# High and low rows of w_up in one matmul of 512 columns, in a hybrid decoder layer on one Trainium2 core

## The chip, the cores and the metric

The kernel runs on one core of one Trainium2 chip. A core has TensorE (matmuls; PE in the profile, PEld for its weight loads), VectorE (DVE), ScalarE (ACT), GpSimd (POOL) and SyncE (SP), each with a queue of its own that it works off in order, and 16 DMA engines. The metric is the device time in microseconds, the median of several runs.

## The reference

One decoder layer for 512 tokens behind 16 meta tokens, model width 2048, in float32:

```
u    = rmsnorm(h, norm_mix)
proj = u @ w_in                        # attention and mLSTM inputs
mix  = [sliding-window attention with sinks | chunkwise mLSTM]
h    = h + mix @ w_out
u    = rmsnorm(h, norm_mlp)
h    = h + square(relu(u @ w_up)) @ w_down     # 2048 -> 8192 -> 2048
out  = rmsnorm(h, norm_final)[without meta tokens]
```

The change is in `u @ w_up`, where each product is 512 tokens x 2048 x 8192.

## The kernel before, in words

**Precision.** TensorE takes operands in fp32r. To keep float32 accuracy each operand is split in a high part (the value cast to fp32r, by ACT, line 118) and a low part (the rest, by DVE, line 119), in `split`. A product a x w is then three matmuls: high by high, low by high, high by low.

**Stages, in order of time.** The input projection (lines 165, 178 to 180, 227), attention and mLSTM between its tiles, w_out (lines 709 to 711, `tok_gemm`), w_up (`up_quad`, lines 755 to 757), w_down (`product` and `step`, lines 1056 to 1060), and the final norm. In w_out and w_down the weights' halves stream through TensorE in 512 columns and activations are the loaded operand; in w_up the weights (`whi`, `wlo`, 128x128 at a time) are loaded and the activations stream.

**w_up.** It is done in 32 quads. A quad takes a 2 x 2 arrangement of blocks and works it with seven products instead of eight (the sums and differences of Strassen's scheme in Winograd's form): the weight sums `s1` to `s4` are made by DVE (`w_sum`, line 735), the activation sums were made before, when the rows were transposed. `ORDER = (0, 1, 5, 4, 6, 2, 3)` is the order of the products. Each product runs over KQ = 8 slices q of 128 rows, with three matmuls of HTOK = 256 columns per slice: `wh` by `yh`, `wh` by `yl`, `wl` by `yh`. Results lie in three PSUM tiles, X, W and Q (W and Q are halves of one bank), and X and Q go on accumulating over several products; ACT copies X or Q out in between, DVE adds, and ACT applies Relu and Square to the tile `d` (four quarters of 256 columns). DVE makes four sums `fs` of d (POOL does so in the last quad), and ACT's queue sends d and fs to DRAM (lines 824, 825). Odd quads use the PSUM tiles named a, even ones g. Quad 0 is written by hand and overlaps with the end of w_out.

**Buffers.** `hi_lo` gives a pair of weight halves from three buffers each (`whi`, `wlo`). The activations yh, yl of j = 0, 1 lie in the pool b2, those of j = 2, 3 in slots of the pool xpool, which are reused: x in the input projection, the attention output in w_out, y in w_up, and the first 16 of 24 places for the units of w_down. A slot is TOK = 528 elements wide. The other 8 places are in the pool b3r (tiles named r). Slots of xpool appear in the profile as s; so do the weight sums of w_up and of w_down, which are also named s.

**w_down.** Units (512-column pieces of d and fs, read back from DRAM, tile fu) are split into high and low halves and used as the loaded operand; the weights come in blocks as raw and rh, with DVE's differences t1 to t4 (`weight_sum`, line 1025). Its pools are opened when those of w_up close, one behind the other in the space that the pool b2 (y tiles, then weight sums) and the pool b2b (d, fs, raws, small ones) leave: b3f (fu, rh), b3r, b3 (the quarters c), b3s (weight sums s).

**Order.** Where nothing else is said, a planner decides the order of instructions on each engine's queue from a priority (the program's order) and a timeline of its own. In `manual_schedule` blocks the program's order stands for the engines named: all of w_down's loop on PE, ACT and DVE. The last product (g = LAST + 12), written in two halves t, stood outside of such a block.

Of the kernel before, what the change touches and what calls it, by code (L numbers as in the profile page):

```python
# [10 lines left out]
F32 = mybir.dt.float32  # L11
F32R = mybir.dt.float32r
AF = mybir.ActivationFunctionType
ALU = mybir.AluOpType
# [69 lines left out]
def hybrid_layer(ctx, tc, io, out):  # L84
# [100 lines left out]
    with tc.tile_pool(name="a0", bufs=1) as a0:  # L185
# [15 lines left out]
        for k0, kn in groups:  # L201
            xr = a0.tile([P, kn, TOK], F32, name=f"xr{k0}")
            wr = (mk[:, :, :SEQ], mq, qa[0], qa[1])[k0 // 4][:, k0 % 4 : k0 % 4 + kn]
            sync.dma_start(out=xr[:], in_=io["xt"][:, k0 : k0 + kn])
            sync.dma_start(out=wr, in_=io["wa"][:, k0 : k0 + kn])
            if k0 == 1:
                sync.dma_start(out=cst[:, KT:], in_=io["cst"][:, KT:])
            for j in range(kn):
                kt = k0 + j
                xh[kt], xl[kt] = xslot(2 * kt, (P, TOK)), xslot(2 * kt + 1, (P, TOK))  # L210
# [365 lines left out]
    def mlstm_block(n):  # L576
# [30 lines left out]
        for h in range(MH):  # L607
            o = abank((P, MV + 1))
            pe.matmul(o[:], e[:, h], ml["v"][:, n, h], start=True, stop=False)
            pe.matmul(o[:], qs[:, h], ml["C"][:, h], start=False, stop=True)  # L610
            act.copy(num[:, h], o[:])
            act.activation(junk[:], num[:, h, :MV], AF.Square, accum_out=ss[:, h : h + 1])
# [64 lines left out]

    ah, al = [None] * KT, [None] * KT
    for kt in range(KT):
        ah[kt], al[kt] = xslot(2 * kt, (P, SEQ)), xslot(2 * kt + 1, (P, SEQ))  # L680
# [35 lines left out]

    b2s = ExitStack()
    b2 = b2s.enter_context(tc.tile_pool(name="b2", bufs=1, reuse_waits="tile"))
    yh, yl = {}, {}
    for p in ORDER:  # L720
        for j in range(2):
            yh[p, j] = b2.tile([P, 2, HTOK], F32R, name=f"yh{p}_{j}")
            yl[p, j] = b2.tile([P, 2, HTOK], F32R, name=f"yl{p}_{j}")

    def sum_tile():
        return b2.tile([P, 1024], F32, name="s", tag="s", bufs=NS_)
# [2 lines left out]
    def operand(src):  # L729
        w = hi_lo()  # L730
        split(w[0][:], w[1][:], src)
        return w
# [4 lines left out]
    def up_quad(quad):  # L737
# [10 lines left out]
        s1, s2, s3, s4 = (sum_tile() for _ in range(4))  # L748
        nb = abank if quad % 2 else bank

        def product(p, w, out, q0=0, q1=KQ, start=True):
            for q in range(q0, q1):
                wh, wl = (t[:, q * P : (q + 1) * P] for t in w)
                ah_, al_ = yh[p, q // 2][:, q % 2], yl[p, q // 2][:, q % 2]
                pe.matmul(out, wh, ah_, start=start and q == 0, stop=False, skip_group_check=True)  # L755
                pe.matmul(out, wh, al_, start=False, stop=False, skip_group_check=True)  # L756
                pe.matmul(out, wl, ah_, start=False, stop=q == KQ - 1, skip_group_check=True)  # L757

        if quad == 0:
            pa, pb, pc = (nb((P, 2, HTOK)) for _ in range(3))  # L760
# [29 lines left out]
            act.activation(d[:], d[:], AF.Relu)  # L790
        else:

            X, B = nb((P, HTOK)), nb((P, 2, HTOK))
            W, Q = B[:, 0], B[:, 1]
            d = b2b.tile([P, 4, HTOK], F32, name="d", bufs=2)
# [4 lines left out]
            product(1, operand(x12), W)  # L800
            product(5, operand(s2[:]), X[:], start=False)
            dve.tensor_tensor(out=d[:, 0], in0=d[:, 0], in1=W, op=ALU.add)  # L802
            act.copy(d[:, 2], X[:])
            product(4, operand(s1[:]), Q)
            w_sum(s3, x11, x21, ALU.subtract)
            act.copy(d[:, 1], Q)
            product(6, operand(s3[:]), X[:], start=False)
            w_sum(s4, x12, s2[:], ALU.subtract)
            act.copy(d[:, 3], X[:])
            product(2, operand(s4[:]), Q, start=False)  # L810
            dve.tensor_tensor(out=d[:, 3], in0=d[:, 3], in1=d[:, 1], op=ALU.add)
            act.activation(d[:, 0], d[:, 0], AF.Relu)
            product(3, operand(x22), X[:], start=False)
            dve.tensor_tensor(out=d[:, 2], in0=d[:, 2], in1=Q, op=ALU.add)
            act.activation(d[:, 2:4], d[:, 2:4], AF.Relu)
            act.activation(d[:, 1], X[:], AF.Relu)
        act.activation(d[:], d[:], AF.Square)
        fs = b2b.tile([P, 4, HTOK], F32, name="fs")
        summer = dve if quad < NQ - 1 else pool
# [9 lines left out]
    with tc.tile_pool(name="b2a", bufs=1, reuse_waits="tile") as b2a:  # L829
        for j in range(NJ):  # L830
# [55 lines left out]
                act.activation(y[:, i], src, AF.Copy, scale=gmlp[:, kt : kt + 1])  # L886
            if j >= 2:
                for i, p in enumerate(ORDER):
                    yh[p, j] = xslot(4 * i + 2 * (j - 2), (P, 2, HTOK))
                    yl[p, j] = xslot(4 * i + 2 * (j - 2) + 1, (P, 2, HTOK))  # L890
# [34 lines left out]
    b3r = []  # L925


    def unit_slot(k, n, shape, dt=F32R):
        k %= UNITS
        if k < 16:  # L930
            i = 2 * XU[k] + n
            return xpool.tile(list(shape), dt, tag=f"s{i}", name=f"s{i}")
        return b3r[0].tile(list(shape), dt, tag=f"r{k}_{n}", name=f"r{k}_{n}")

    keys_ = [(c, p, h) for c in range(NC) for p in ORDER for h in range(2)]
    loaded, unit = {}, {}
# [4 lines left out]
        sync.dma_start(out=buf[:].rearrange("p (a b) -> p a b", a=2), in_=fdram[2 * c + h][pos // 4][:, pos % 4])  # L941

    def split_unit(k, buf):
        unit[keys_[k]] = hi, lo = [unit_slot(k, n, (P, 512)) for n in range(2)]
        split(hi[:], lo[:], buf[:])

    def early_unit(buf):
        k = len(loaded)
# [25 lines left out]


    b3f = ctx.enter_context(tc.tile_pool(name="b3f", bufs=1, reuse_waits="tile"))
    b3r.append(ctx.enter_context(tc.tile_pool(name="b3r", bufs=1, reuse_waits="tile")))
    b3 = ctx.enter_context(tc.tile_pool(name="b3", bufs=1, reuse_waits="tile"))
    b3s = ctx.enter_context(tc.tile_pool(name="b3s", bufs=1, reuse_waits="tile"))
    dps = ctx.enter_context(tc.tile_pool(name="dps", bufs=1, space=PSUM, reuse_waits="tile"))  # L980

    def f_buffer():
# [123 lines left out]
            sync.dma_start(out=nfs[j][:], in_=io["nf"][:, j * 512 : (j + 1) * 512])  # L1106

    def load_h1(row, j):
        for b in (2 * row, 2 * row + 1):
            h1[b, j] = unit_slot(len(keys_) + 2 * j + b // 2, b % 2, (P, 512), F32)[:]  # L1110
            sync.dma_start(out=h1[b, j], in_=hd[j][row][:, b % 2])

    def load_quarter(row, col):
# [4 lines left out]

    def squares(row, j):
        for b in (2 * row, 2 * row + 1):  # L1120
            square_sum(junk[:], b, j, h1[b, j])

    def weigh(row, j):
        for b in (2 * row, 2 * row + 1):
# [58 lines left out]

    def last_square(b, j):
        last_sq[b] = b3.tile([P, 1], F32, name=f"sq{b}")
        act.activation(junk[:], h1[b, j], AF.Square, accum_out=last_sq[b][:])

    load_units(FB)
    load_rows0(0, 0)
    load_rows0(0, 1)  # L1190
    load_rows1(0)
    junk = unit_slot(len(keys_) + 2 * NJ, 0, (P, 512), F32)
# [108 lines left out]
```

## Time and profile before

| what | value |
|---|---|
| median of 3 runs | 2002.85 us (2001.46 to 2003.85) |
| the profiled execution | 1999.89 us, its span 1998.1 us |
| granted TensorE clock, mean | 0.996 |
| PE busy | 1971.5 us, 99% of the span, 12240 matmuls |
| DVE busy | 1405.5 us, 70% |
| ACT busy | 1011.1 us, 51% |
| POOL busy | 236.0 us, 12% |
| w_up, quads 1 to 31 | 735 us to 1358 us from the span's start |
| w_down | 1358 us to the end |

Matmuls are pipelined: a row of one lasts longer than the time until the next begins, so the price of a matmul is the time from start to start. A group's row reads: line, engine, operation, written tile <- read tiles, shape, count, then busy us, mean ns of one, idle us ahead of it and who ended that. A row of the timeline reads: start, duration, engine, line, operation, tiles, shape, and in brackets the idle time ahead of it with its releaser. A row of waits reads: who waited, for whom, us in total, times, the longest.

### The profile page before, as it was taken

The numbers are of one execution on the slowest core, as the hardware profiler recorded it, in microseconds if no ns is written. First come the engines' busy times: TensorE is split into PE (matmuls) and PEld (weight loads), VectorE is DVE, ScalarE is ACT, GpSimd is POOL, SyncE is SP. The second block draws the span as 40 slices with busy tenths as digits, with TensorE's granted clock in tenths as the row PEclk, the third lists the DMA queues.
The fourth block names the chain that finished last, engine by engine and source line by source line (L and its number), as shares of the span: only waits on it lengthen the run. The fifth ranks groups of instructions, "written<-read, shape, count | busy, mean of one in ns | idle before, by whom it ended". The sixth has DMA issues, their size and how long they took to land.

```text
span 1998.1 us, 30652 instructions
## 1 busy us (share of the span) xinstructions
PE 1971.5 (99%) x12240; PEld 1754.5 (88%) x12240; DVE 1405.5 (70%) x1844; ACT 1011.1 (51%) x1491; POOL 236.0 (12%) x341
## 2 busy tenths in 40 slices
PE   9999999999999999999999999998999999999997
PEld 7878889988888889999999999997888888888886
DVE  6557673233643478877777777776888888888878
ACT  4433552235533355555555555555566565555655
POOL 0112220012120023122220000000100000010011
PEclk9999999999999999999999999999999999999999
DMA  8412112221343336555554444456887887787766
GB/s 313 132 64 87 64 64 85 85 85 64 106 148 129 108 146 208 192 183 187 183 186 158 161 156 162 156 167 216 206 223 211 227 222 211 218 216 194 219 170 188
DMA packets 113392, 324.61 MB, mean 162 GB/s; under 512 B 14016, under 2 KB 51008, under 8 KB 94288
## 3 DMA queue, kind: packets, MB, share of 16 engines
q1 hardware_dynamic: 66304, 246.60, 36.1%
q0 software_dynamic: 11856, 40.38, 10.6%
q10 hardware_dynamic: 35088, 35.66, 5.5%
q8 instruction: 96, 1.57, 0.3%
q14 instruction: 48, 0.39, 0.1%
HBM read 244.45 MB, written 78.15 MB: 161 GB/s over the span
## 4 chain that ended last, share of the span: by engine, by line
PE 90%; issue 4%; DVE 2%; DMA 1%; ACT 1%; POOL 1%; DVEq 0%; SPq 0%; POOLq 0%; ACTq 0%
PE g L165 10%; PE a L755 5%; PE a L757 5%; PE a L756 5%; PE g L755 5%; PE g L757 5%; PE g L756 5%; PE X L1056 5%; PE X L1060 5%; PE X L1059 5%; PE g L709 3%; PE g L711 3%; PE g L710 3%; PE Q L1060 2%; PE Q L1056 2%
## 5 line engine op out<-in xcount | busy, mean ns | idle before, releaser
L118 ACT CAST whi<-raw 128x1024 fp32r<-128x1024 f32 x224 | 234.9, 1049 | 412.3 <-PE g L711 89.6
L119 DVE TENSOR_TENSOR wlo<-raw,whi 128x1024 fp32r<-128x1024 f32 x224 | 274.2, 1225 | 207.1 <-ACT whi L118 201.8
L119 DVE TENSOR_TENSOR wlo<-s,whi 128x1024 fp32r<-128x1024 f32 x256 | 312.9, 1223 | 121.6 <-ACT whi L118 119.5
L118 ACT CAST whi<-s 128x1024 fp32r<-128x1024 f32 x256 | 268.7, 1050 | 224.8 <-PE g L756 64.1
L165 PE MATMUL g<-s,whi 128*128 128x264 f32 x1216 | 205.1, 287 | 0.2 <-DVE qa L263 0.2
L165 PEld LDWEIGHTS g<-s,whi 128*128 128x128 f32 x1216 | 171.0, 189 | 5.4 <-issue 4.9
L1060 PE MATMUL X<-whi,s 128*128 128x512 f32 x356 | 140.2, 394 | 0.0
L1056 PE MATMUL X<-whi,s 128*128 128x512 f32 x356 | 140.0, 393 | 0.0
L1059 PE MATMUL X<-wlo,s 128*128 128x512 f32 x356 | 139.8, 393 | 0.0
L165 PE MATMUL g<-s,wlo 128*128 128x264 f32 x608 | 128.0, 287 | 0.0
L755 PE MATMUL a<-yh,whi 128*128 128x256 f32 x448 | 126.5, 282 | 1.5 <-DVE d L802 0.8
L755 PE MATMUL g<-yh,whi 128*128 128x256 f32 x448 | 126.7, 283 | 1.2 <-ACT whi L118 1.1
L757 PE MATMUL a<-yh,wlo 128*128 128x256 f32 x448 | 126.4, 282 | 0.6 <-DVE wlo L119 0.6
L757 PE MATMUL g<-yh,wlo 128*128 128x256 f32 x448 | 126.2, 282 | 0.0
L755 PE MATMUL a<-s,whi 128*128 128x256 f32 x448 | 126.1, 282 | 0.0
L756 PE MATMUL g<-yl,whi 128*128 128x256 f32 x448 | 126.1, 281 | 0.0
L756 PE MATMUL a<-yl,whi 128*128 128x256 f32 x448 | 126.1, 281 | 0.0
L755 PE MATMUL g<-s,whi 128*128 128x256 f32 x448 | 125.8, 282 | 0.0
L757 PE MATMUL a<-s,wlo 128*128 128x256 f32 x448 | 125.7, 280 | 0.0
L757 PE MATMUL g<-s,wlo 128*128 128x256 f32 x448 | 125.6, 281 | 0.0
L756 PE MATMUL a<-s,whi 128*128 128x256 f32 x448 | 125.5, 280 | 0.0
L756 PE MATMUL g<-s,whi 128*128 128x256 f32 x448 | 125.4, 280 | 0.0
(367 smaller groups left out, 5114.0 us busy)
## 6 DMA issues: line engine op xcount, KB each, us to landing
raw<-in_w_dram SPq DMA_DIRECT2D x144, 1024.0 KB, 5.1
rh<-in_w_dram SPq DMA_DIRECT2D x64, 512.0 KB, 5.3
hd<-c POOLq DMA_DIRECT2D x61, 512.0 KB, 5.5
fu<-fd SPq DMA_DIRECT2D x110, 256.0 KB, 3.5
fd<-d ACTq DMA_DIRECT2D x32, 512.0 KB, 3.2
fd<-fs ACTq DMA_DIRECT2D x32, 512.0 KB, 3.5
xtok<-in_x_dram SPq DMA_DIRECT2D x4, 1024.0 KB, 11.5
hs<-in_x_dram SPq DMA_DIRECT2D x16, 256.0 KB, 6.0
```

The lines of the kernel that those rows point to most:

```text
L118: act.copy(dst_hi, src)
L119: dve.tensor_tensor(out=dst_lo, in0=src, in1=dst_hi.bitcast(F32), op=ALU.subtract)
L165: pe.matmul(ps[s][:], w, x[:, s * HALF : (s + 1) * HALF], start=first and kt == 0, stop=last and kt == KT - 1,)
L709: pe.matmul(ps[b][:], a, wh, start=kt == first, stop=False)
L710: pe.matmul(ps[b][:], a, wl, start=False, stop=False)
L711: pe.matmul(ps[b][:], c, wh, start=False, stop=kt == last)
L755: pe.matmul(out, wh, ah_, start=start and q == 0, stop=False, skip_group_check=True)
L756: pe.matmul(out, wh, al_, start=False, stop=False, skip_group_check=True)
L757: pe.matmul(out, wl, ah_, start=False, stop=q == KQ - 1, skip_group_check=True)
L1056: pe.matmul(out[:, t], a, wh[:, cols], start=start and h == q == 0, stop=False, skip_group_check=True)
L1059: pe.matmul(out[:, t], a, wl[:, cols], start=False, stop=False, skip_group_check=True)
L1060: pe.matmul(out[:, t], a2, wh[:, cols], start=False, stop=h == q == 1, skip_group_check=True)
```

## The change

Slots for high and low halves become one tile with both (`xpair`, `unit_pair`, `y_pair`): one tile of [128, 2, n] per pair. For y it is `[P, 2, 2, HTOK]` (half, slice, token), so that one access pattern reads a slice's high and low rows as two runs of 256 columns. In quads 1 to 31 `wide` streams both in one matmul of 512 columns for `wh`; `wl` still takes the high rows alone. The result of a product is then two halves of one bank, and X, W and Q are a bank each. `snapshot` copies both halves out (tile e), and DVE adds the halves, partly ahead of and partly behind the other sums. The early Relus of single quarters become one Relu over all of d. The tile d has one buffer instead of two, e has two of half its size. The pool b3s is opened right behind b3f instead of last. The last product's two halves are in a `manual_schedule` block for PE.

```diff
-    def xslot(i, shape):
-        return xpool.tile(list(shape), F32R, tag=f"s{i}", name=f"s{i}")
+    def xpair(i, shape, dt=F32R):
+        t = xpool.tile([P, 2] + list(shape), dt, tag=f"s{i}", name=f"s{i}")
+        return t[:, 0], t[:, 1]
...
+    def y_pair(p, j, pool_, **kw):
+        ys[p, j] = t = pool_.tile([P, 2, 2, HTOK], F32R, **kw)
+        yh[p, j], yl[p, j] = t[:, 0], t[:, 1]
...
-        def product(p, w, out, q0=0, q1=KQ, start=True):
+        def product(p, w, out, q0=0, q1=KQ, start=True, wide=False):
             for q in range(q0, q1):
                 wh, wl = (t[:, q * P : (q + 1) * P] for t in w)
...
+                if wide:
+                    pe.matmul(
+                        out[:], wh, ys[p, q // 2][:, :, q % 2], start=start and q == 0, stop=False,
+                        skip_group_check=True,
+                    )
+                    pe.matmul(out[:, 0], wl, ah_, start=False, stop=q == KQ - 1, skip_group_check=True)
...
-            X, B = nb((P, HTOK)), nb((P, 2, HTOK))
-            W, Q = B[:, 0], B[:, 1]
-            d = b2b.tile([P, 4, HTOK], F32, name="d", bufs=2)
-            product(0, operand(x11), X[:])
-            act.copy(d[:, 0], X[:])
+            X, W, Q = (nb((P, 2, HTOK)) for _ in range(3))
+            d = b2b.tile([P, 4, HTOK], F32, name="d")
+            def snapshot(src):
+                e = b2b.tile([P, 2, HTOK], F32, name="e", bufs=2)
+                act.copy(e[:], src[:])
+                return e
...
+            wide(0, x11, X)
+            e0 = snapshot(X)
             w_sum(s1, x21, x22, ALU.add)
             w_sum(s2, s1[:], x11, ALU.subtract)
...
+            wide(1, x12, W)
+            wide(5, s2[:], X, False)
+            add(e0[:], e0[:], W[:])
+            e2 = snapshot(X)
+            wide(4, s1[:], Q)
             w_sum(s3, x11, x21, ALU.subtract)
...
+            add(d[:, 0], e0[:, 0], e0[:, 1])
+            act.copy(d[:, 1], Q[:, 0])
+            add(d[:, 1], d[:, 1], Q[:, 1])
+            wide(6, s3[:], X, False)
             w_sum(s4, x12, s2[:], ALU.subtract)
...
+            e3 = snapshot(X)
+            wide(2, s4[:], Q, False)
+            add(d[:, 3], e3[:, 0], e3[:, 1])
+            add(d[:, 3], d[:, 3], d[:, 1])
+            wide(3, x22, X, False)
+            add(e2[:], e2[:], Q[:])
+            add(d[:, 2], e2[:, 0], e2[:, 1])
+            act.copy(d[:, 1], X[:, 0])
+            add(d[:, 1], d[:, 1], X[:, 1])
+            act.activation(d[:], d[:], AF.Relu)
         act.activation(d[:], d[:], AF.Square)
...
     b3f = ctx.enter_context(tc.tile_pool(name="b3f", bufs=1, reuse_waits="tile"))
+    b3s = ctx.enter_context(tc.tile_pool(name="b3s", bufs=1, reuse_waits="tile"))
     b3r.append(ctx.enter_context(tc.tile_pool(name="b3r", bufs=1, reuse_waits="tile")))
     b3 = ctx.enter_context(tc.tile_pool(name="b3", bufs=1, reuse_waits="tile"))
-    b3s = ctx.enter_context(tc.tile_pool(name="b3s", bufs=1, reuse_waits="tile"))
...
-        product(LAST + 12, (t,), (0, 1))
+        with tc.manual_schedule(engines=MAN):
+            product(LAST + 12, (t,), (0, 1))
```

More of the change, by code (lines that the diff above doesn't have):

```diff
@@ L718, in hybrid_layer @@
     b2 = b2s.enter_context(tc.tile_pool(name="b2", bufs=1, reuse_waits="tile"))
[L719 removed]
+    ys, yh, yl = {}, {}, {}
+    def y_pair(p, j, pool_, **kw):
+        ys[p, j] = t = pool_.tile([P, 2, 2, HTOK], F32R, **kw)
+        yh[p, j], yl[p, j] = t[:, 0], t[:, 1]
     for p in ORDER:
         for j in range(2):
[L722 to L723 removed]
+            y_pair(p, j, b2, name=f"y{p}_{j}")
     def sum_tile():
@@ L749, in up_quad @@
         nb = abank if quad % 2 else bank
-        def product(p, w, out, q0=0, q1=KQ, start=True):
+        def product(p, w, out, q0=0, q1=KQ, start=True, wide=False):
             for q in range(q0, q1):
                 wh, wl = (t[:, q * P : (q + 1) * P] for t in w)
[L754 to L757, printed above, removed]
+                ah_ = yh[p, q // 2][:, q % 2]
+                if wide:
[4 more added lines that the diff above has]
+                    pe.matmul(out[:, 0], wl, ah_, start=False, stop=q == KQ - 1, skip_group_check=True)
+                else:
+                    pe.matmul(out, wh, ah_, start=start and q == 0, stop=False, skip_group_check=True)
+                    pe.matmul(out, wh, yl[p, q // 2][:, q % 2], start=False, stop=False, skip_group_check=True)
+                    pe.matmul(out, wl, ah_, start=False, stop=q == KQ - 1, skip_group_check=True)
         if quad == 0:
@@ L791, in up_quad, with wide @@
         else:
-            X, B = nb((P, HTOK)), nb((P, 2, HTOK))
-            W, Q = B[:, 0], B[:, 1]
-            d = b2b.tile([P, 4, HTOK], F32, name="d", bufs=2)
-            product(0, operand(x11), X[:])
-            act.copy(d[:, 0], X[:])
+            X, W, Q = (nb((P, 2, HTOK)) for _ in range(3))
+            d = b2b.tile([P, 4, HTOK], F32, name="d")
+            def wide(p, src, out, start=True):
+                product(p, operand(src), out, start=start, wide=True)
+            def snapshot(src):
+                e = b2b.tile([P, 2, HTOK], F32, name="e", bufs=2)
+                act.copy(e[:], src[:])
+                return e
@@ L798, in up_quad, with add @@
+            def add(dst, in0, in1):
+                dve.tensor_tensor(out=dst, in0=in0, in1=in1, op=ALU.add)
+            wide(0, x11, X)
+            e0 = snapshot(X)
             w_sum(s1, x21, x22, ALU.add)
             w_sum(s2, s1[:], x11, ALU.subtract)
[L800 to L804, printed above, removed]
+            wide(1, x12, W)
@@ L810, in up_quad @@
[L810 to L816, printed above, removed]
+            e3 = snapshot(X)
+            wide(2, s4[:], Q, False)
@@ L925, in hybrid_layer, with unit_pair @@
     b3r = []
-    def unit_slot(k, n, shape, dt=F32R):
+    def unit_pair(k, dt=F32R):
         k %= UNITS
         if k < 16:
-            i = 2 * XU[k] + n
-            return xpool.tile(list(shape), dt, tag=f"s{i}", name=f"s{i}")
-        return b3r[0].tile(list(shape), dt, tag=f"r{k}_{n}", name=f"r{k}_{n}")
+            return xpair(XU[k], (512,), dt)
+        t = b3r[0].tile([P, 2, 512], dt, tag=f"r{k}", name=f"r{k}")
+        return t[:, 0], t[:, 1]
     keys_ = [(c, p, h) for c in range(NC) for p in ORDER for h in range(2)]
@@ L943, in split_unit @@
     def split_unit(k, buf):
-        unit[keys_[k]] = hi, lo = [unit_slot(k, n, (P, 512)) for n in range(2)]
-        split(hi[:], lo[:], buf[:])
+        unit[keys_[k]] = hi, lo = unit_pair(k)
+        split(hi, lo, buf[:])
     def early_unit(buf):
```

21 lines of the change are left out of this document (9 added, 12 removed).

## The prediction

> **What bounds the kernel now.** I read the page first, then the table by stretches, then the waits inside the w_up stretch, then single rows.
>
> ```profile
> span 1998.1 us, 30652 instructions
> PE 1971.5 (99%) x12240; PEld 1754.5 (88%) x12240; DVE 1405.5 (70%) x1844; ACT 1011.1 (51%) x1491; POOL 236.0 (12%) x341
> PE 90%; issue 4%; DVE 2%; DMA 1%; ACT 1%; POOL 1%; DVEq 0%; SPq 0%; POOLq 0%; ACTq 0%
> ```
>
> TensorE (PE) carries 90% of the chain that ended last, so what shortens its stream shortens the run, as long as no other engine takes over. The table by stretches says where that could happen (start:end, length, then busy time of PE, weight load, DVE, ACT, POOL, granted clock):
>
> ```profile
> 735.00:764.00 29.00, 26.92 (x220) 26.12 (x219) 26.79 (x35) 16.07 (x22) 16.09 (x8) 1.00 0.45 152
> 764.00:1358.00 594.00, 593.82 (x4995) 593.61 (x4994) 459.45 (x533) 318.80 (x447) 62.27 (x86) 1.00 0.52 176
> 1358.00:1372.00 14.00, 6.50 (x28) 5.04 (x27) 5.88 (x8) 6.94 (x10) 2.87 (x4) 0.87 0.40 113
> ```
>
> The middle row is w_up: 594.00 us over 4995 matmuls is 118.9 ns from one to the next, with no holes. A quad has 7 products x 8 slices x 3 = 168 matmuls, so it lasts 19.98 us; 594.00 holds 29.73 quads. In each, DVE is busy 459.45/29.73 = 15.45 us and idle 4.52. Is that idle time slack or need? The waits of the same stretch answer:
>
> ```profile
> DVE wlo L119 <- ACT whi L118: 116.9, 119, 1.9
> ACT whi L118 <- PE g L756: 107.5, 75, 1.9
> ACT whi L118 <- PE a L756: 107.2, 74, 1.6
> ```
>
> DVE waits for ACT's casts, and ACT for PE to give back a weight buffer: 116.9 of DVE's 134.5 us idle is PE's own pace. It can be filled.
>
> **The change part by part.**
>
> *w_up in 512 columns.* In quads 1 to 31 each slice goes from three matmuls of 256 columns to one of 512 (wh over high and low rows together) and one of 256 (wl over high): 31 x 7 x 8 = 1736 slices. w_down already runs 512 columns, here with weights from the tiles r and from s:
>
> ```profile
> 1411.85 0.40 PE L1056 MATMUL W<-whi,s 128*128 128x512 f32 x1
> ...
> 1417.39 0.40 PE L1056 MATMUL X<-whi,s 128*128 128x512 f32 x1
> 1500.00 0.39 PE L1056 MATMUL Q<-whi,r 128*128 128x512 f32 x1
> ...
> 1510.88 0.39 PE L1056 MATMUL Q<-whi,s 128*128 128x512 f32 x1
> ```
>
> From 1411.85 to 1417.39 is one product of 24 matmuls: 230.8 ns each. From 1500.00 to 1510.88 are 48: 226.7 ns. Twice 118.9 is 237.8, so a 512 in place of two 256 saves 7.0 to 11.1 ns. In w_up the loaded weights are whi and wlo, the same in all slices, and half of the rows lie in plain tiles, half in s; I take 228, nearest to the r rows. A slice then costs 228 + 118.9 = 346.9 instead of 356.7, a quad 19.43, and 1736 x 9.8 ns = **-17.1 us** (-12.2 to -19.3).
>
> The Trainium skill, "TensorE: Matmul & The Clock Gate", section Back-to-back issue gap, gives N/2.4 + 2.5 ns for a warm matmul by itself; that is 109.2 and 215.8 ns, so joining would save 2.5 ns a slice, an estimated 4.3 us in place of 17.1. The trace does not agree with it: a 256 takes 118.9 here, so more than that rule's fixed part goes when one instruction goes.
>
> *Halves added on leaving PSUM.* ACT and DVE pay. Three DVE adds of 256 columns per quad (L802, L811, L814) become two of 512 and six of 256. Rows of quad 0 have both sizes, two of them reading PSUM; the cost in the queue is from start to start:
>
> ```profile
> 741.96 0.41 DVE L788 TENSOR_TENSOR d<-fs,g 128x256 f32<-128x256 f32 x1
> 742.29 0.68 DVE L789 TENSOR_TENSOR d<-fs,g 128x512 f32<-128x512 f32 x1
> 742.89 0.41 DVE L802 TENSOR_TENSOR d<-d,a 128x256 f32<-128x256 f32 x1
> 743.22 1.21 DVE L119 TENSOR_TENSOR wlo<-s,whi 128x1024 fp32r<-128x1024 f32 x1
> L118 ACT CAST whi<-s 128x1024 fp32r<-128x1024 f32 x118 | 124.1, 1051 | 128.8 <-PE g L756 63.1 <-PE a L756 61.8
> L119 DVE TENSOR_TENSOR wlo<-s,whi 128x1024 fp32r<-128x1024 f32 x118 | 144.3, 1223 | 70.1 <-ACT whi L118 68.2
> L815 ACT ACTIVATE d<-d 128x512 f32<-128x512 f32 x30 | 18.8, 626 | 0.0
> L812 ACT ACTIVATE d<-d 128x256 f32<-128x256 f32 x30 | 12.6, 419 | 8.1 <-DVE d L802 8.1
> L816 ACT ACTIVATE d<-g 128x256 f32<-128x256 f32 x15 | 5.7, 377 | 0.0
> L809 ACT COPY d<-a 128x256 f32<-128x256 f32 x15 | 5.5, 364 | 0.0
> L817 ACT ACTIVATE d<-d 128x1024 f32<-128x1024 f32 x29 | 30.8, 1061 | 0.9
> ```
>
> 256 columns cost 0.33, 512 cost 0.60. So 2 x 0.60 + 6 x 0.33 = 3.18 against 0.99: +2.2 us. DVE goes to 17.65 of a quad of 19.43, 91%, with 1.78 us left. ACT: three copies of 512 at about 0.63 (L815's size), two of 256 at 0.36 and a Relu of 1024 at 1.06 in place of four copies of 256 and Relus of 0.42, 0.63 and 0.38: +0.8 on 318.80/29.73 = 10.7 us. Both stay under PE, so in the steady state I cost them at nothing; DVE's cover is the 1.78 us. Three weight buffers help: a buffer is cast when PE leaves it, two products (5.5 us) before its next use, and cast plus subtraction take 1.05 + 1.22 us, so DVE may come 3.2 us late before PE feels it. New waits of PE are those of X and Q: each is copied or added out while another product of 2.8 us runs.
>
> *One d instead of two.* The quad's first write to d must now wait until the last quad's d has gone to DRAM:
>
> ```profile
> 1015.63 0.28 PE L755 MATMUL a<-yh,whi 128*128 128x256 f32 x1
> 1020.22 1.06 ACT L817 ACTIVATE d<-d 128x1024 f32<-128x1024 f32 x1
> 1021.42 0.52 ACTq L824 DMA_DIRECT2D fd<-d  x1
> DMA to landing us min/median/max: 3.2/3.2/5.2
> POOL fs L820 <- ACT d L817: 316.7, 1, 316.7
> ```
>
> The next quad's products began at 1015.63 (the tile names turn from g to a), so the issue of d comes 5.8 us in. The new end of a quad (copy 0.36, add 0.42, whole Relu 1.06 in place of the last Relu of 0.38) makes it 7.3, landing at 10.5. The first sum into d is ready at about 6.5: DVE can block there for up to 4 us if the planner puts that add early, with lo parts queued behind it. Q's copy into d comes at 11.1, so ACT just passes. Price 0 if the add is planned late, up to 1 us a quad if not; I take 0, since the planner sees the wait. The start is different: in the first row of the stretches (quads 0 to 1) DVE has 2.2 us free in 29 and PE already lost 2.1. There the extra 2.2 us falls on the path: **+2** (0 to +4), with the two early units' later fd inside it. POOL's scalings of res, which queue ahead of the last quad's sums there, may take longer beside a busier DVE; POOL then stood idle for 316.7 us, which covers them.
>
> *Pools of w_down.* The third row above is the change of stage; the rows in it:
>
> ```profile
> 1366.12 1.22 DVE L1025 TENSOR_TENSOR s<-raw 128x1024 f32<-128x1024 f32 x1 [8.56 <-DMA fd<-fs]
> 1362.84 3.21 DMA fd<-fs
> 1361.22 1.05 ACT L118 CAST whi<-rh 128x1024 fp32r<-128x1024 f32 x1
> 1363.58 0.40 PE L1056 MATMUL W<-whi,s 128*128 128x512 f32 x1
> 1371.48 0.79 PE L1059 MATMUL W<-wlo,s 128*128 128x512 f32 x1 [7.50 <-DVE wlo L119]
> 1375.33 0.39 PE L1059 MATMUL W<-wlo,s 128*128 128x512 f32 x1
> ```
>
> The first weight sum s waits until fs of the last quad has been stored: s stood last in the stack, at 78 KB above b2's start, on fs (76 to 80). Everything behind it on DVE waits too, the wlo among it, so PE idles 7.50 us; then nine matmuls take 3.85 us (1371.48 to 1375.33) instead of 9 x 0.231, +1.8, with the clock granted 0.87 over the stretch. Moved behind b3f, s lies at 30 to 50 KB, on y tiles of p = 4, 6, 2, 3, which PE is done with by the end of its last product. What is late next: the cast of rh, behind the longer end of the quad on ACT (+1.45), so 1362.7 to 1363.7, its wlo at 1364.9, and PE wants it at 1363.8. A stall of 1.1 us stays, and DVE may lag by up to 1.8 in the steps after it. 7.50 + 1.8 - 1.1 = 8.2 at best, 6.4 with the lag: **-7** (0 to -9.3). fs's old place now holds units r, first split a block later, and the quarters c lie on the raws.
>
> *Pairs.* A unit's low half lay 528 x 4 = 2112 bytes behind the high one in s; now it is 2048, as it was in r, and the same for the attention output in w_out. The two streams above differ by 230.8 - 226.7 = 4.1 ns, for 1920 matmuls in w_down and 768 in w_out: 11 us if the distance is the cause, 0 if it is where s lies; a loss has no row, I allow 2. Slots of s still step by 4224 bytes and r by 2048, so only part of it is mended: **-4**, nearer to nothing.
>
> *Last product pinned in order.* Its two halves, into W and X, end together now:
>
> ```profile
> 1984.10 0.40 PE L1060 MATMUL W<-whi,s 128*128 128x512 f32 x1
> 1985.26 0.39 PE L1060 MATMUL X<-whi,s 128*128 128x512 f32 x1
> ```
>
> In program order W's half would end 12 matmuls (2.8 us) before the other, 1.6 sooner than now; DVE and POOL have work behind each half, but the last half decides: **-0.5** (0 to -1.5).
>
> Sum: -17.1 + 2 - 7 - 4 - 0.5 = **-26.6 us**. The profiled execution took 1999.89 us (span 1998.1), 2.96 under the median of 2002.85; from the median the result is 1976.
>
> **The rivals.**
>
> *DVE takes over (the other side).* One mechanism: in-order waits of DVE, at the adds that need PE's end of a product and at d's store, do not shrink while its work grows. A quad costs 17.65 plus the idle that stays. It breaks even on its own at 19.98 - 17.65 = 2.33 us of idle, and with the 9.5 us that the other parts give back (0.3 a quad) at 2.64. With 3.0 kept a quad is 20.65: +20.8 - 9.5, 2014 us. With all of today's 4.52 it is 22.17: 2061. For it: 91% load and the single d. Against: the 116.9 us that are PE's pace.
>
> *Joined columns save nothing.* If a 512 over two runs of 256 takes twice 118.9, the first term is 0: 1993 us. For it: no row streams two runs. Against: 226.7 and 230.8 for one run. The skill's gap rule named above would land beside it, at an estimated 1989 us.
>
> *The stall between the stages only changes its name* (another tile of the new order, or POOL's sums, which ACT waits for before it can issue their store): the -7 is 0, 1983 us.
>
> **How the numbers follow.** Forecast as summed: 0.60, by itself 1965 to 1987 (all bounds good at once would be -41, 1962; the other end has the smaller joining, -12.2, the start at +4 and no gain of the pairs, 1987). Nothing saved by joining: 0.13. Stall renamed: 0.12. DVE takes over: 0.15, of which 0.10 ends slower, 0.02 the same, 0.03 still faster. 0.2% (4 us) is what a measurement tells from no change here. Faster: 0.60 + 0.12 + 0.11 + 0.03 = 0.86; same 0.02 + 0.02 = 0.04; slower 0.10. The range 1963 to 1995 leaves out the slow side of the DVE case and single ends of the others, about 0.19.
>
> **What would show it.** Right: in the w_up stretch about 347 ns per pair of a 512 and a 256 and quads of 19.4 us; DVE near 17.6 us of each, its waits still for ACT's whi; no wait of 7 us at W and no clock under 1.00 around the change of stage; s rows in w_down below 230. Wrong: PE rows in w_up that wait for wlo, or DVE rows that wait for fd<-d, in every quad; the 512 rows at 238 ns; a new releaser named at the first w_down products.

## The result and the profile after

The changed kernel takes 2054.79 us (median; 2052.33 to 2061.25) against 2002.18 us of the kernel before in the same session (2001.46 to 2003.85): a ratio of 1.0269, interval 1.0252 to 1.0286. It is slower by 53 us, where 27 us less were forecast. The profiled execution took 2056.31 us, 56.4 more than the one of before; the two spans differ by as much.

The page of the changed kernel has these lines for the three shown first of before (span; busy time and count of each engine; the chain that ended last):

```profile
span 2054.5 us, 27414 instructions
PE 1983.2 (97%) x10504; PEld 1671.1 (81%) x10504; DVE 1472.7 (72%) x1999; ACT 1031.8 (50%) x1460; POOL 234.4 (11%) x341
PE 71%; DVE 9%; issue 9%; DMA 5%; ACT 4%; POOL 1%; ACTq 0%; DVEq 0%; SPq 0%; POOLq 0%
```

PE fell from 90% to 71% of the chain, and DVE, issue, DMA and ACT took its place. The table by stretches says where:

```profile
735.00:764.00 29.00, 23.77 (x120) 19.19 (x119) 25.32 (x32) 13.02 (x16) 7.67 (x10) 0.94 0.44 141
764.00:1358.00 594.00, 550.45 (x3033) 467.76 (x3032) 477.55 (x623) 309.03 (x381) 67.97 (x84) 0.99 0.50 157
```

A changed quad has 7 x 8 x 2 = 112 matmuls, so the second row holds 594.00 / (3033/112) = 21.93 us per quad, against 19.98 before and 19.43 forecast. (By the issues of d's store most quads last 21.5 us, the 21.48 of the expectations below; six of 23.6 to 24.5 us raise the mean.) PE's busy time now leaves 43.5 us of the stretch open, where it left 0.2. All the loss lies in w_up: by the starts of its first and last matmuls, quads 1 to 31 took 622.7 us before and 683.7 after (+61.0); what follows, up to the end of the span, went from 640.2 to 635.1 (-5.1).

The waits from 800 to 1350 us (who waited, for whom, total, times, longest) name a new releaser:

```profile
ACT d L831 <- DMA fd<-d: 36.7, 22, 3.5
PE a L762 <- ACT whi L119: 17.9, 12, 3.0
PE g L762 <- ACT whi L119: 15.8, 13, 1.8
```

These 550 us hold 25 quads: in 22 of them ACT waits for the store of d, and about once in each PE waits for a cast of ACT. One quad's boundary, in the timeline, shows how the two hang together:

```profile
1014.15 1.06 ACT L845 ACTIVATE d<-d 128x1024 f32<-128x1024 f32 x1
1015.24 0.52 ACTq L852 DMA_DIRECT2D fd<-d  x1
1015.25 9.04 SPq L749 DMA_DIRECT2D raw<-in_w_dram  x2
...
1021.25 0.42 DVE L851 TENSOR_TENSOR fs<-d,fs 128x256 f32<-128x256 f32 x1
1021.70 0.52 ACTq L853 DMA_DIRECT2D fd<-fs  x1
1022.50 0.37 ACT L831 COPY d<-a 128x256 f32<-128x256 f32 x1 [1.40 <-DMA fd<-d]
1022.88 1.04 ACT L119 CAST whi<-raw 128x1024 fp32r<-128x1024 f32 x1
1023.98 0.50 PE L762 MATMUL g<-y,whi 128*128 128x512 f32 x1 [1.06 <-ACT whi L119]
1024.66 0.50 PE L762 MATMUL a<-y,whi 128*128 128x512 f32 x1 [0.17 <-DVE d L818]
```

The store of d is issued in the same instant as the loads of the raw weights, and lands 7.2 us later, at 1022.4. Q's copy into d (L831) cannot start before, and it holds ACT's queue: behind it stands the cast for a product that PE is ready to begin. PE idles 1.06 us for that cast and 0.17 us for the sum into d; the rest of a quad's loss is in shorter waits that were not taken apart. The landing is not alone in this. The last fs sum (L851), which also reads d, is done only 0.8 us before the store has landed; the store of fs, which waits for that sum, stands ahead of the copy in ACT's queue, and its issue ends at 1022.22. Without the landing the copy could have come only 0.3 us sooner.

### The profile page after: what moved, and what is told of

It is laid out like the page before. It is cut to its first block, busy times and chain, and to the rows that moved or that the text cites. A ratio compares the mean times of both kernels' runs of the same rounds, so it can differ in the third digit from the quotient of the medians.

```text
span 2054.5 us, 27414 instructions
## 1 busy us (share of the span) xinstructions
PE 1983.2 (97%) x10504; PEld 1671.1 (81%) x10504; DVE 1472.7 (72%) x1999; ACT 1031.8 (50%) x1460; POOL 234.4 (11%) x341
## 4 chain that ended last, share of the span: by engine, by line
PE 71%; DVE 9%; issue 9%; DMA 5%; ACT 4%; POOL 1%; ACTq 0%; DVEq 0%; SPq 0%; POOLq 0%
PE g L166 9%; PE a L762 6%; PE X L1084 4%; PE X L1088 4%; PE X L1087 4%; PE g L762 4%; DMA fd<-d 4%; DVE wlo L120 3%; PE g L710 3%; PE g L712 3%; PE g L711 3%; PE a L766 3%; DVE s L740 2%; PE Q L1084 2%; PE Q L1088 2%
## 5 line engine op out<-in xcount | busy, mean ns | idle before, releaser
L762 PE MATMUL a<-y,whi 128*128 128x512 f32 x448 | 166.4, 407 | 25.1 <-ACT whi L119 22.8
L762 PE MATMUL g<-y,whi 128*128 128x512 f32 x420 | 157.7, 411 | 24.7 <-ACT whi L119 19.0
L762 PE MATMUL a<-s,whi 128*128 128x512 f32 x448 | 163.2, 397 | 0.0
L762 PE MATMUL g<-s,whi 128*128 128x512 f32 x420 | 152.3, 396 | 0.0
L766 PE MATMUL a<-y,wlo 128*128 128x256 f32 x448 | 126.2, 282 | 1.4 <-DVE wlo L120 1.4
L762 PEld LDWEIGHTS a<-y,whi 128*128 128x128 f32 x448 | 83.5, 189 | 51.2 <-ACT whi L119 28.4
L762 PEld LDWEIGHTS g<-y,whi 128*128 128x128 f32 x420 | 79.5, 192 | 49.6 <-ACT whi L119 23.7
L766 PE MATMUL g<-y,wlo 128*128 128x256 f32 x420 | 119.4, 284 | 0.0
L1094 POOL DMA_DIRECT2D hd<-c x60 | 51.8, 864 | 525.9 <-DVE c L1091 472.8
L762 PEld LDWEIGHTS a<-s,whi 128*128 128x128 f32 x448 | 84.7, 189 | 20.7
```

Source lines behind the costliest of these rows:

```text
L762: pe.matmul(out[:], wh, ys[p, q // 2][:, :, q % 2], start=start and q == 0, stop=False, skip_group_check=True,)
L766: pe.matmul(out[:, 0], wl, ah_, start=False, stop=q == KQ - 1, skip_group_check=True)
L1094: pool.dma_start(out=hd[2 * BLOCKS[B][1] + col][row][:], in_=cs[B, f"c{row}{col}"][:], accum_op=ALU.add)
```

## The experiments

### The version that stores fs in d's place

> Part changed: the store that should send d to DRAM sends the sums fs a second time, so half of the units hold fs's numbers instead of d's; the traffic is the same, but no one waits for d's store any more. Theory S (the single d: its store is issued late and lands late, ACT's copy of Q into d waits for it, and the next cast waits behind that copy): ACT's waits for fd<-d are gone, quads go from 21.48 to about 19.8 us and the run to about 2000 us (1990 to 2012). Theory D (DVE at over 80% of a quad with in-order waits of its own): quads stay above 21 us and the run at 2040 to 2060.

```diff
-        act.dma_start(out=fdram[quad // 2][0][:, :, quad % 2], in_=d[:])
+        act.dma_start(out=fdram[quad // 2][0][:, :, quad % 2], in_=fs[:])
```

It took 2049.36 us in the one run that was made, 5 less than the changed kernel's median, where Theory S had some 2000. ACT's wait for the store of d is gone from the list, yet a quad still lasts 576.00 / (2983/112) = 21.63 us in the mean, and most of them 21.4 to 21.7 as in the changed kernel. The stretch 764 to 1340, and the place in the timeline that answers to the one above:

```profile
764.00:1340.00 576.00, 532.80 (x2983) 456.53 (x2981) 472.93 (x618) 304.59 (x377) 77.19 (x84) 1.00 0.47 159
...
1035.98 0.42 DVE L851 TENSOR_TENSOR fs<-d,fs 128x256 f32<-128x256 f32 x1
...
1036.44 0.52 ACTq L852 DMA_DIRECT2D fd<-fs  x1
1037.00 0.65 ACTq L853 DMA_DIRECT2D fd<-fs  x1
1037.75 0.37 ACT L831 COPY d<-g 128x256 f32<-128x256 f32 x1 [1.92 <-PE g L766]
1038.02 1.05 ACT L119 CAST whi<-raw 128x1024 fp32r<-128x1024 f32 x1
...
1039.12 0.50 PE L762 MATMUL a<-y,whi 128*128 128x512 f32 x1 [1.47 <-ACT whi L119]
```

Both stores now wait for L851 in ACT's queue, the copy comes 0.1 us after the second one's issue has ended (1037.00 + 0.65), and the cast that PE needs next still stands behind it. (The bracket at the copy names PE, but the last matmul of the product into Q started at 1034.58, three us earlier.) So the landing alone isn't the holder, and Theory S as it was put is refuted (the expectation for two d's widens it), while Theory D's numbers are met in this run: what costs is that the copy stands ahead of the cast and is released late, by whatever reader of d comes last, the store or DVE's last sum with the store of fs behind it.

### DVE relieved

> Part left out: three of DVE's adds per quad (W to the first copy, Q's low half, and the sum of quarters 3 and 1), 1.3 us of DVE time; the single d, the end of a quad and the stores stay. Theory D: quads lose at least that 1.3 us, run at 2015 or below. Theory S: the store of d and ACT's wait for it are where they were, quads stay within 0.4 us of 21.48, run at 2040 to 2060.

```diff
-            add(e0[:], e0[:], W[:])
...
-            add(d[:, 1], d[:, 1], Q[:, 1])
...
-            add(d[:, 3], d[:, 3], d[:, 1])
```

The three additions are worth 0.60 + 2 x 0.33 = 1.26 us of DVE a quad. The one run took 2017.61 us, 37 less and between the two forecasts. The stretch 764 to 1340 and the waits from 800 on:

```profile
764.00:1340.00 576.00, 560.06 (x3121) 480.09 (x3120) 456.44 (x560) 311.65 (x392) 55.96 (x83) 0.99 0.52 167
...
ACT d L830 <- DMA fd<-d: 94.8, 24, 5.5
DVE d L818 <- DMA fd<-d: 45.1, 26, 3.3
```

A quad lasts 576.00 / (3121/112) = 20.67 us, shorter by 1.26, just what was taken off DVE. By itself that would speak for Theory D, though the edit also leaves out a sum that PE waits for before it writes Q again. A less busy DVE finishes its fs sums earlier (3.7 us after the issue of d's store in one quad, against 6.4), and the waiting moves to the store: ACT now waits 4 us a quad for it, and DVE 1.7. So DVE's fullness makes the wait dearer: in the changed kernel L851 comes late, and the copy with it. Whether it is the origin this run can't tell; the next ones take away the wait and leave DVE full.

### Only the pools reordered

> The kernel before with b3s opened right behind b3f, and nothing else. Theory of the prediction (the weight sums lay on fs and waited for its store): the wait of 8.6 us of DVE for fd<-fs and PE's 7.5 us are gone, 5 to 8 us faster (ratio 0.9960 to 0.9975). Rival (the stall is only renamed: ACT waits for POOL's sums before it can issue their store, with the casts behind): below 3 us.

```diff
+    b3s = ctx.enter_context(tc.tile_pool(name="b3s", bufs=1, reuse_waits="tile"))
     b3r.append(ctx.enter_context(tc.tile_pool(name="b3r", bufs=1, reuse_waits="tile")))
     b3 = ctx.enter_context(tc.tile_pool(name="b3", bufs=1, reuse_waits="tile"))
-    b3s = ctx.enter_context(tc.tile_pool(name="b3s", bufs=1, reuse_waits="tile"))
```

In the kernel before this gives 1994.74 us, a ratio of 0.9963 (0.9951 to 0.9976): -7.4 us. The term of the prediction was -7.

### Q copied into a third e, d still single

> The changed kernel, but Q is copied into a third tile e instead of into d (the early unit shares e's buffers, so no more memory is used), and DVE adds it to e3; ACT then never waits for d's store. Theory S: ACT's wait for fd<-d is gone and no cast is held up, quads near 19.8 us, run at 1995 to 2010, perhaps with some of DVE's own wait for d left. Theory D: quads above 21 us, run at 2040 to 2060.

```diff
-                e = b2b.tile([P, 2, HTOK], F32, name="e", bufs=2)
+                e = b2b.tile([P, 2, HTOK], F32, name="e", tag="e", bufs=3)
...
-            act.copy(d[:, 1], Q[:, 0])
-            add(d[:, 1], d[:, 1], Q[:, 1])
+            e1 = snapshot(Q)
...
+            add(e3[:], e3[:], e1[:])
             add(d[:, 3], e3[:, 0], e3[:, 1])
-            add(d[:, 3], d[:, 3], d[:, 1])
```

(The early units share the tag e, for the space.) 1990.07 us, a ratio of 0.9946 (0.9931 to 0.996): 65 us less than the changed kernel, with one d as there, and 5 less than Theory S allowed.

```profile
735.00:764.00 29.00, 26.27 (x144) 21.61 (x143) 27.32 (x34) 15.56 (x20) 9.76 (x11) 1.00 0.42 142
764.00:1340.00 576.00, 576.00 (x3272) 501.21 (x3271) 510.32 (x646) 339.53 (x411) 73.01 (x83) 1.00 0.56 175
...
DVE d L818 <- DMA fd<-d: 0.8, 2, 0.4
```

PE has no hole left in 576 us, a quad lasts 19.72 us, and DVE works 510.32 / (3272/112) = 17.47 us of it, 89%. The store still takes 7.6 us in the median; nothing that matters waits for it now.

### Two d's again, and its control

> The changed kernel with two buffers of d as before; the room comes from w_up's weight sums (two buffers instead of three, s4 written over s2). Theory S, widened (ACT's copy of Q into the one d waits for d's readers, the store and DVE's last sum fs, and the cast behind it and the next product into Q wait for that copy): ACT's copy of Q waits for PE alone, quads of 19.6 to 20.0 us, run at 1985 to 2005. Theory D (DVE's load, whatever the buffers): quads above 21 us, run at 2040 to 2060.

> The control of the run with two d: only the weight sums have two buffers, d stays single. Both theories: the sums' third buffer hides nothing that matters, run at 2045 to 2070; if it comes out near 2000, the order of DVE's sums and not d's buffers was the cause.

```diff
-NS_ = 3
+NS_ = 2
...
-            w_sum(s4, x12, s2[:], ALU.subtract)
+            w_sum(s2, x12, s2[:], ALU.subtract)
...
-            d = b2b.tile([P, 4, HTOK], F32, name="d")
+            d = b2b.tile([P, 4, HTOK], F32, name="d", bufs=2)
```

A second d (in both places where d is made) only fits if one of the weight sums' buffers goes. The control has the sums' edit alone. With both edits 1999.79 us (0.9993, 0.9983 to 1.0002); the control 2086.74 us in one run, so that edit helps nothing by itself: it costs 32 us, more than the 2045 to 2070 that were expected. Between the two, d's second buffer alone is worth 87 us. The stretch 764 to 1340, with two d's and from 900 to 1300 by itself, and then the control:

```profile
764.00:1340.00 576.00, 568.53 (x3198) 492.62 (x3197) 504.00 (x662) 324.62 (x403) 63.13 (x83) 0.99 0.54 172
900.00:1300.00 400.00, 400.00 (x2269) 347.21 (x2268) 356.17 (x466) 229.82 (x284) 27.75 (x42) 1.00 0.54 172
```

```profile
764.00:1340.00 576.00, 520.65 (x2768) 445.84 (x2768) 442.23 (x573) 281.68 (x347) 59.46 (x83) 0.95 0.48 151
```

With two d's PE's holes in it, 7.5 us, are two waits for a cast before 900 us; from 900 to 1300 PE has none, with DVE busy 89% of the time. They make up most of the 10 us to the version with Q in e. In the control, from 800 to 1340, DVE's sums into d wait 51.8 us for the store of d and a copy of ACT 43.1, and PE waits 50.7 us for sums of DVE.

### High and low rows side by side

> The kernel with Q copied into e, and y laid out so that a slice's high and low rows lie side by side (one run of 512 columns instead of two of 256 with a gap). If the gap is what makes w_up's 512 take 233 to 235 ns against 227 of w_down's r rows: 512 at 227 to 229 ns, quads from 19.7 to 19.4 us, run 9 to 12 us below the 1990.07 of the kernel without it (1978 to 1981). If the price is that of streaming y at all: 233 to 235 ns, the same time within 3 us.

```diff
-        yh[p, j], yl[p, j] = t[:, 0], t[:, 1]
+        yh[p, j], yl[p, j] = t[:, :, 0], t[:, :, 1]
...
-                        out[:], wh, ys[p, q // 2][:, :, q % 2], start=start and q == 0, stop=False,
+                        out[:], wh, ys[p, q // 2][:, q % 2], start=start and q == 0, stop=False,
```

On top of the version with Q in e, a 512 reads one run of 512 columns, not two of 256. 1989.41 us (0.9945, 0.9928 to 0.9962). From start to start (gaps over 300 ns, and over 150 ns at a 256, are left out of this and all such means below) a 512 took 235.1 ns on y and 234.3 on s in the mean, to the tenth what it took without the edit: two runs cost nothing here.

### The kernel before with one d

> The kernel before with one buffer of d, nothing else. Its store is issued about 2.7 us after the quad's last product and lands in 3.2. If the single d alone is enough to stall: more than 2015 us, with ACT's first copy into d waiting for fd<-d. If it needs the longer end of the quad and the halves' adds: within 8 us of 2002.

```diff
-            d = b2b.tile([P, 4, HTOK], F32, name="d", bufs=2)
+            d = b2b.tile([P, 4, HTOK], F32, name="d")
```

2058.69 us in one run, +57 from this edit alone (made in both places where d is). The stretch, and the place in a quad:

```profile
764.00:1340.00 576.00, 537.84 (x4449) 532.02 (x4448) 418.51 (x482) 285.88 (x400) 58.50 (x81) 1.00 0.47 159
...
1010.28 0.52 ACTq L824 DMA_DIRECT2D fd<-d  x1
1013.13 1.05 ACT L118 CAST whi<-s 128x1024 fp32r<-128x1024 f32 x1 [1.80 <-PE a L756]
1014.08 0.37 ACT L797 COPY d<-a 128x256 f32<-128x256 f32 x1
1014.50 0.39 PE L755 MATMUL a<-yh,whi 128*128 128x256 f32 x1 [1.29 <-ACT d L797]
```

A quad lasts 576.00 / (4449/168) = 21.75 us. The store is quick here, 3.2 us in the median, and has landed at 1013.5; the copy comes 0.6 us after that because it stands behind a cast, which itself waits for PE. Here it is the first copy, X into d, that PE needs: from 800 to 1340 PE waits 32.9 us for it. The expectation had the time, but not the name of the wait; ACT's wait at that copy for the store itself shows only twice, 1.9 us in all, as the cast in front covers the rest. So one d costs about as much with DVE at 418.51/576 = 73%: the loss doesn't need DVE to be full.

### 512s and 256s apart

> This is the version with Q's two halves copied into a third tile e, with one more edit: in each product of w_up the eight matmuls of 512 columns run first and the eight of 256 after them, instead of 512 and 256 by turns. TensorE has hardly any idle time in w_up there, so the stream's own price shows. In that version a 512 took 234.3 to 235.1 ns and a 256 117.3 to 117.8, where the prediction had taken 228 and 118.9. Theory A, the turn from one length to the other costs the difference: the 512 falls to 227 to 231 ns, so 1736 x 4 to 8 ns = 7 to 14 us less, 1977 to 1984 us. Theory B, the price comes from the operands and not from the order: both prices stay within 1 ns, time within 3 us of 1990. Either way wlo is wanted 1.9 us later in each product, which can only ease DVE.

```diff
-                    pe.matmul(
-                        out[:], wh, ys[p, q // 2][:, :, q % 2], start=start and q == 0, stop=False,
-                        skip_group_check=True,
-                    )
-                    pe.matmul(out[:, 0], wl, ah_, start=False, stop=q == KQ - 1, skip_group_check=True)
...
+                for q in range(q0, q1):
+                    pe.matmul(
+                        out[:], wh[:, q * P : (q + 1) * P], ys[p, q // 2][:, :, q % 2],
+                        start=start and q == 0, stop=False, skip_group_check=True,
+                    )
+                for q in range(q0, q1):
+                    pe.matmul(
+                        out[:, 0], wl[:, q * P : (q + 1) * P], yh[p, q // 2][:, q % 2],
+                        start=False, stop=q == KQ - 1, skip_group_check=True,
+                    )
```

1987.77 us, 0.9926 (0.991 to 0.9943). One product in the timeline, four matmuls to a row:

```profile
1101.12 1.07 PE L760 MATMUL a<-y,whi 128*128 128x512 f32 x4
1102.03 1.07 PE L760 MATMUL a<-s,whi 128*128 128x512 f32 x4
1102.94 0.63 PE L765 MATMUL a<-y,wlo 128*128 128x256 f32 x4
1103.40 0.64 PE L765 MATMUL a<-s,wlo 128*128 128x256 f32 x4
1103.88 1.07 PE L760 MATMUL a<-y,whi 128*128 128x512 f32 x4
```

Eight 512s take 1102.94 - 1101.12 = 1.82 us, 227.5 ns each, and eight 256s 0.94 us, 117.5 each. Over all of w_up the means are 228.2 and 228.4 (y, s) and 116.8 and 119.2. On the price Theory A holds: by turns with a 256 a 512 is 6 to 7 ns dearer than in a group. The edit also takes whi and wlo in groups as loaded weights, and no run separates that from the lengths. On the time Theory A misses: the median is 2.3 us lower than that of the version with Q in e, which was measured in another session, and by the profiled executions quads 1 to 31 took 615.6 us with the edit and without. New stalls of PE came in for the gain, the longest being these:

```profile
769.50 1.20 PE L760 MATMUL g<-y,whi 128*128 128x512 f32 x4 [1.81 <-ACT e L819]
850.59 1.20 PE L760 MATMUL g<-y,whi 128*128 128x512 f32 x4 [1.63 <-ACT e L819]
1346.54 1.20 PE L760 MATMUL a<-y,whi 128*128 128x512 f32 x4 [3.11 <-ACT e L819]
```

The last is the single d again: DVE's first sum into d waits 5.06 us for the store, and ACT's copy of e for that sum. At the change of stage PE waits 3.3 us at W in two stalls, the longer 2.8, against 3.7 in three without the edit.

### The last quad's sums on DVE

> The version with Q in a third tile e, and the last quad's four sums fs on DVE, not on POOL. In that version, at the change from w_up to w_down, POOL's sums take 1.41, 1.71, 0.73 and 0.74 us, the weight difference of rh on DVE beside them takes 1.60 us instead of 1.22, and three stalls of TensorE at W add up to 3.7 us. Theory A, what is left of the stall comes from POOL's sums (ACT waits for them ahead of their store's issue, and DVE is slower beside them): the stalls fall to 2 us or less, total 1988 us or less. Theory B, the stalls come from the longer end of the quad on ACT and from DVE's queue, which now gets 4 x 0.33 = 1.3 us more: no gain, 1990 to 1993 us.

```diff
-        summer = dve if quad < NQ - 1 else pool
+        summer = dve
```

1986.48 us, 0.9921 (0.9906 to 0.9936), the lowest median of all, though its interval overlaps those of the versions next to it. The weight difference of rh at the change of stage, first in the version without the edit, beside POOL's sum, then with it:

```profile
1356.01 1.60 DVE L120 TENSOR_TENSOR wlo<-rh,whi 128x1024 fp32r<-128x1024 f32 x1
1356.48 1.71 POOL L849 TENSOR_TENSOR fs<-d 128x256 f32<-128x256 f32 x1
```

```profile
1356.03 1.22 DVE L120 TENSOR_TENSOR wlo<-rh,whi 128x1024 fp32r<-128x1024 f32 x1
```

The stalls at W named for wlo stay (2.4 us in two, 2.3 before), the 1.4 us one named for whi is gone, and from w_up's last matmul to the end 634.1 us pass instead of 636.8. ACT's wait for the sums is shorter, 3.15 us for DVE in place of 4.33 for POOL. Theory A is right for part of what was left, not for all of it.

### Both together

> Both last edits together: Q's halves in a third tile e, eight 512s ahead of eight 256s in each product, and the last quad's sums on DVE. If the two gains are of different places they add: by turns to grouped gave -2.3 us in the medians, the sums on DVE -3.6, so 1984. Rival: the grouped order lost two thirds of its 12 us in a few single stalls (3.1 us in the last quad where DVE's first sum into d waits for d's store, 1.8 and 1.6 in early quads) and lagged at the change of stage (2.8 us at W); with the sums on DVE, DVE's queue is fuller there, and the lag stays: 1987 or more.

1987.31 us, 0.9926 (0.991 to 0.9943): the gains don't add, as the rival had it; the interval does not tell it from either edit alone. Against the sums on DVE alone quads 1 to 31 are 2.3 us shorter (613.7) and what follows is 2.2 longer (636.3): what the grouped order saves in the stream comes back as a wait at the change of stage.

## Why the prediction was wrong

**The step that failed** is "One d instead of two", priced at 0 with "Q's copy into d comes at 11.1, so ACT just passes", and beside it the sentence that X and Q's waits are covered because "each is copied or added out while another product of 2.8 us runs". Measured, the quad lost 21.93 - 19.72 = 2.2 us, 31 times 68 us; the kernel before loses 57 us to the single d alone. Four things were taken wrongly in it.

- *The store's landing.* 3.2 us was taken from a page on which the raw loads were issued 3.8 us behind the store. Its issue now falls together with theirs. The page after has

```profile
fd<-d ACTq DMA_DIRECT2D x32, 512.0 KB, 7.2
```

  (issues, size, median us to landing). With 7.2 in the prediction's own sum, landing is at 14.5, 3.4 us behind the copy at 11.1. The row of 3.2/3.2/5.2 carried no warning. A right landing would not have saved the forecast, though: with nobody waiting for it a quad still lasted 21.63 us, and the kernel before with one d loses as much at a landing of 3.2.
- *The other readers of d.* The prediction let the first write to d wait for the store alone. DVE's last fs sum reads d too, late in a full queue, and the store of fs behind it stands in ACT's queue ahead of the copy; in the quad shown that issue ends 0.2 us ahead of the landing.
- *What stands behind the copy.* The bound of 1 us a quad was made for DVE's adds. The copy on ACT has the next cast behind it, and PE waits for that cast. DVE's queue was looked through for what would be stuck; ACT's wasn't. From 764 to 1358 in the changed kernel DVE's waits for the store come to 0.8 us; ACT's, from 800 to 1350 alone, to 36.7.
- *"Since the planner sees the wait".* The planner put the copy ahead of the cast and the wait into ACT's queue. In the kernel before with one d it put a cast ahead of the copy instead; there PE waited for the copy itself, and the whole was as dear.

**The rival "DVE takes over"** gave 2061 with all of DVE's 4.52 us of idle kept, and it was on the right side at 2055, but that it came so near is luck. With Q in e, or with two d's, DVE works 89% of each quad and PE has no hole, so the load alone costs nothing; with DVE relieved the loss shrinks and doesn't go. Its bound, in-order waits at d's store, was right; the place was ACT's queue, with DVE's last sum as one of the things it waits for. Only in the control with two sums did PE wait for DVE's sums in nearly every quad.

**Joined columns.** -17.1 was taken from 228 for a 512; in the changed kernel it took 235.0 (y) and 233.2 (s), and a 256 117.4 and 118.0. A pair is 351.8 instead of 346.9, so the term is 1736 x (356.7 - 351.8) = -8.5. The row it was taken from, r in w_down, has 512s only. Where w_up has them in groups they cost 228, as taken. The rival that nothing is saved is refuted, and so is its mechanism of two runs. The Trainium skill's gap rule for a matmul by itself ("TensorE: Matmul & The Clock Gate", Back-to-back issue gap) gives an estimated 215.8 and 109.2 ns for these lengths. The traces do not agree with it: no group of them in these runs averaged below 226.5 and 116.8, and it has no term for mixed lengths.

**Pools of w_down.** The -7 measured -7.4 in the kernel before, with a stall of 2.3 us left where 1.1 was taken. In the changed kernel the stretch behind w_up gave 5.1, the part of the stall that stays being 3.7 us instead of 1.1:

```profile
1424.58 1.60 DVE L120 TENSOR_TENSOR wlo<-rh,whi 128x1024 fp32r<-128x1024 f32 x1
1425.06 1.71 POOL L850 TENSOR_TENSOR fs<-d 128x256 f32<-128x256 f32 x1
1426.24 0.51 PE L1087 MATMUL W<-wlo,s 128*128 128x512 f32 x1 [0.72 <-DVE wlo L120]
1428.88 0.62 ACT L119 CAST s<-fu 128x512 fp32r<-128x512 f32 x1 [4.33 <-POOL fs L851]
1430.49 0.49 PE L1084 MATMUL W<-whi,s 128*128 128x512 f32 x1 [1.48 <-ACT whi L119]
1432.54 0.50 PE L1087 MATMUL W<-wlo,s 128*128 128x512 f32 x1 [1.55 <-DVE wlo L120]
```

The rival "stall renamed", by POOL's sums, was half right: PE's stall of 7.50 us, behind the store of fs, went, and ACT's wait of 4.33 us for POOL came. The Trainium skill ("SBUF — State Buffer", Who interferes with whom) says that a DVE instruction with two SBUF inputs contends with a GpSimd instruction that reads SBUF, by an exclusive lock. The trace agrees that the two slow each other: the same difference takes 1.22 us alone and 1.60 beside POOL, and POOL's sum 1.71 where the next takes 0.73. That a lock does it no run here shows.

**Pairs.** -4 was 0. The three rows of w_down with an s operand, from start to start, were 231.6, 230.1 and 231.7 ns before and 232.6, 229.9 and 231.0 after, with r at 227 in both. The distance between a unit's halves isn't the cause.

**Last product.** -0.5 was 0. Its last rows of W and X still end together, 1.16 us apart as before:

```profile
2041.11 0.39 PE L1088 MATMUL W<-whi,s 128*128 128x512 f32 x1
2042.27 0.40 PE L1088 MATMUL X<-whi,s 128*128 128x512 f32 x1
```

The order of the last 60 matmuls is the same in both traces, W's and X's in alternate groups. The sum took it that all of W's would come first; the two blocks, one for each half, did not bring that about, and why isn't known.

**The start.** In the first row of stretches 120 matmuls of 175.9 ns (half a pair) fill 21.1 of 29 us, 7.9 lost, against 2.8 before; the version with Q in e loses 3.7 there (144 matmuls). So +2 was too little with the single d's wait and near right without it, +0.9.

**The account**, between the profiled executions: forecast -26.6, measured +56.4, apart by 83. Some 68 are the quad's new wait, 8.6 the price of a 512, 6.4 the stages behind w_up, where 11.5 were forecast and 5.1 came.

## What to carry to other kernels

When a tile's second buffer goes, look up the last readers of the old content, the first instruction that writes it again on each engine, and what that engine's queue holds behind it: the price isn't the wait, it is the late start of what stands behind. Read a transfer's landing at the time at which it will now be issued, beside the loads that start then. And a matmul's price read where lengths are uniform need not hold where they alternate: group by length and measure.

## What the runs showed of the hardware

A 512-column matmul that alternates with a 256 took 233 to 235 ns in w_up, and 228 in groups of eight on the same operands, tiles and access pattern, with weights loaded for each in both; in w_down, among its like, it took 227 (r) and 230 to 233 (s). So the order decided in w_up. Why isn't settled, nor whether it is the turn of the lengths or that of the loaded tiles. A 512 KB store landed 3.2 us after issue (median) where the raw loads were issued 3.8 us behind it, and 7.0 to 9.4 us after when it was issued within 1 us of a load of raw weights (30 of the 32 stores of d in the changed kernel); no run changes that time alone.
